# A matmul with bias and residual: own semaphores in one section, and one weight load for two matmuls

## The chip, the cores and the metric

The kernel runs on one core of a Trainium2 chip. The metric is the device time of one execution in microseconds (us); lower is better. Each kernel was run several times. A profiled execution also gives a span: the time from its first to its last instruction on the core. A difference of 2% (4.2 us here) or more is called faster or slower; anything less is "same".

## The reference

```python
batch, m, k, n = 16, 512, 1024, 768        # x and residual, weight and bias: random float32
def reference(x, weight, bias, residual):
    return (np.matmul(x, weight) + bias + residual).astype(np.float32)
```

That is 8192 rows of x, 64 tiles of 128 rows. In float32, x is 33.6 MB, the residual and the output are 25.2 MB each and the weight is 3.1 MB. So 87 MB have to move whatever the kernel does.

## The kernel before

Each tile of x is cast to bfloat16 by ScalarE (ACT). The TensorE (PE) transposes it in four pieces, with pairs of bfloat16 seen as one float32 word. VectorE (DVE) copies the transposed tile from PSUM to `XT`. Then 16 matmuls follow: eight slices of K, each with two column parts of W, 512 and 256 columns wide. GpSimd (POOL) adds the bias to the residual, and VectorE adds the PSUM result to that. All transfers are issued by SyncE (SP) on one queue.

```python
def mm(t, n0, nl, q, e):                        # called for both column parts, n0 = 0 and 512
    K_(nc.tensor.matmul(
        PO[t % HEAD][:, n0:n0 + nl], lhsT=XT[t % XT_N][:, q, :, e],
        rhs=w_sb[:, q, e, n0:n0 + nl],
        start=(q == 0 and e == 0), stop=(q == n_q - 1 and e == 1),
    ))
# ... cut ...
for t in range(HEAD, n_t):
    cast(t + 2)
    pool_adds(t + 1)
    transp(t + 1)
    if t < n_t - 1:
        for q in range(n_q):
            for e in range(2):
                for n0, nl in chunks:
                    mm(t, n0, nl, q, e)
    finish(t - 1)
    pool_adds(t + 1)
```

`nc.tensor.matmul` emits a weight load (of `lhsT`, the slice of x) and a matmul. So the same slice of x is loaded twice in a row, once for each column part. `K_` only keeps the order of the program; the framework sets all waits and semaphores. The framework also shares eight semaphores among all DMAs, so the ninth DMA waits until the first has landed.

## Time and profile before

| | kernel before |
|---|---|
| time, median of 3 runs | 211.56 us (211.50 to 211.57) |
| profiled run: time, span | 210.12 us, 208.3 us |
| TensorE matmul busy, weight loads busy | 97%, 62% |
| DMA engines busy, mean rate | 98.1%, 419 GB/s |
| granted TensorE clock | 0.996 |

"Busy" of the TensorE counts overlapping matmuls once, so 97% doesn't tell whether the matmuls are as dense as they can be. That has to be read from their spacing. PEld, the weight loads, is a row of its own because loads run beside matmuls. The lines are shown in the prediction below. Note that the profiled run (210.12 us) was 1.4 us quicker than the three timed ones; this turned out to matter.

### The profile page before, as it was taken

The numbers are of one execution on the slowest core, as the hardware profiler recorded it, in microseconds if no ns is written. First come the engines' busy times: TensorE is split into PE (matmuls) and PEld (weight loads), VectorE is DVE, ScalarE is ACT, GpSimd is POOL, SyncE is SP. The second block draws the span as 40 slices with busy tenths as digits, with TensorE's granted clock in tenths as the row PEclk, the third lists the DMA queues.
The fourth block names the chain that finished last, engine by engine and source line by source line (L and its number), as shares of the span: only waits on it lengthen the run. The fifth ranks groups of instructions, "written<-read, shape, count | busy, mean of one in ns | idle before, by whom it ended". The sixth has DMA issues, their size and how long they took to land.

```text
span 208.3 us, 3115 instructions
## 1 busy us (share of the span) xinstructions
PE 201.8 (97%) x1298; PEld 130.1 (62%) x1298; DVE 104.7 (50%) x140; ACT 66.1 (32%) x69; POOL 116.0 (56%) x72
## 2 busy tenths in 40 slices
PE   7899999999999999999999999999999999999991
PEld 2455666666666666666666666666666666666651
DVE  0457555445545544654554454555445545544542
ACT  2444513403640272420370094230092046430000
POOL 2100029759999905999029702999207950599500
PEclk9999999999999999999999999999999999999998
DMA  6999999999989999999999999999999999999995
GB/s 233 427 429 436 424 432 457 388 446 421 495 383 466 405 423 427 434 426 415 425 465 418 422 436 452 415 437 406 434 446 451 409 419 475 428 396 444 416 368 221
DMA packets 4927, 87.24 MB, mean 419 GB/s; under 512 B 557, under 2 KB 685, under 8 KB 1841
## 3 DMA queue, kind: packets, MB, share of 16 engines
q1 hardware_dynamic: 4913, 87.05, 98.1%
q8 instruction: 10, 0.16, 0.3%
q14 instruction: 4, 0.03, 0.0%
HBM read 61.88 MB, written 25.17 MB: 418 GB/s over the span
## 4 chain that ended last, share of the span: by engine, by line
PE 92%; DMA 4%; DVE 1%; SPq 0%; ACT 0%; issue 0%
PE psum_o L164 78%; PE pt L157 13%; DMA x_tile<-in_x_dram 4%; PE psum_o L258 1%; DVE xt L158 0%; ACT xb L146 0%; DVE ro L262 0%; SPq L119 0%; SPq L122 0%
## 5 line engine op out<-in xcount | busy, mean ns | idle before, releaser
L164 PE MATMUL psum_o<-w_sb,xt 128*128 128x512 bf16 x1008 | 174.0, 326 | 0.5 <-DVE xt L158 0.3
L164 PEld LDWEIGHTS <-xt 128*128 128x128 bf16 x1008 | 98.5, 98 | 59.2 <-DVE xt L158 0.7
L189 POOL TENSOR_TENSOR ro<-ro,bias_sb 128x768 f32<-128x768 f32 x50 | 88.9, 1823 | 48.2 <-DMA ro<-in_residual_dram 37.7
L149 ACT CAST xb<-x_tile 128x1024 bf16<-128x1024 f32 x60 | 59.7, 1043 | 113.9 <-DMA x_tile<-in_x_dram 74.1
L158 DVE COPY xt<-pt 128x1024 bf16<-128x1024 bf16 x64 | 44.1, 691 | 84.4 <-PE pt L157 84.4
L199 DVE TENSOR_TENSOR ro<-psum_o,ro 128x768 f32<-128x768 f32 x49 | 46.5, 948 | 4.6 <-POOL ro L189 3.4
L185 POOL TENSOR_TENSOR ro<-ro 128x768 f32<-128x768 f32 x14 | 25.0, 1820 | 25.0 <-DMA ro<-in_residual_dram 25.0
L157 PE MATMUL pt<-ident,xb 128*128 128x128 f32 x256 | 38.3, 273 | 0.6 <-DVE xb L149 0.4
L157 PEld LDWEIGHTS pt<-ident,xb 128*128 128x128 f32 x256 | 29.7, 140 | 9.0 <-ACT xb L146 1.1
L195 DVE TENSOR_TENSOR ro<-psum_o,bias_sb 128x768 f32<-128x768 f32 x14 | 13.2, 947 | 0.0
L208 PE MATMUL psum_o<-warm 128*128 128x512 bf16 x12 | 4.8, 587 | 1.2 <-DVE warm_a L204 1.2
L229 ACT CAST w_sb<-ro 128x768 bf16<-128x768 f32 x4 | 3.3, 832 | 3.7 <-DMA ro<-in_weight_dram 3.7
L208 PEld LDWEIGHTS <-warm 128*128 128x128 bf16 x12 | 1.6, 141 | 3.9 <-issue 2.7
L229 POOL CAST w_sb<-ro 128x768 bf16<-128x768 f32 x1 | 0.8, 824 | 5.5 <-DMA ro<-in_weight_dram 5.5
L149 DVE CAST xb<-x_tile 128x1024 bf16<-128x1024 f32 x1 | 0.7, 694 | 4.5 <-DMA x_tile<-in_x_dram 4.5
L146 ACT CAST xb<-x_tile 128x512 bf16<-128x512 f32 x3 | 1.8, 617 | 3.4 <-PE psum_o L164 1.7
L258 PE MATMUL psum_o<-w_sb,xt 128*128 128x512 bf16 (+1 forms) x16 | 2.8, 326 | 0.0
L229 DVE CAST w_sb<-ro 128x768 bf16<-128x768 f32 x3 | 1.7, 556 | 2.0 <-DMA ro<-in_weight_dram 2.0
L147 DVE CAST xb<-x_tile 128x512 bf16<-128x512 f32 x3 | 1.2, 424 | 2.6 <-DMA x_tile<-in_x_dram 2.6
L258 PEld LDWEIGHTS <-xt 128*128 128x128 bf16 x16 | 1.6, 98 | 1.1
L223 PE MATMUL psum_o<-warm 128*128 128x512 bf16 x6 | 1.6, 379 | 0.0
L262 DVE TENSOR_TENSOR ro<-psum_o,ro 128x512 f32<-128x512 f32 (+1 forms) x2 | 1.1, 557 | 0.9 <-PE psum_o L258 0.8
(14 smaller groups left out, 5.1 us busy)
## 6 DMA issues: line engine op xcount, KB each, us to landing
out_dram<-ro SPq DMA_DIRECT2D x3, 6144.0 KB, 34.1
x_tile<-in_x_dram SPq DMA_DIRECT2D x3, 5120.0 KB, 24.1
ro<-in_residual_dram SPq DMA_DIRECT2D x3, 3840.0 KB, 25.3
x_tile<-in_x_dram SPq DMA_DIRECT2D x3, 3072.0 KB, 40.2
ro<-in_residual_dram SPq DMA_DIRECT2D x3, 2304.0 KB, 17.5
x_tile<-in_x_dram SPq DMA_DIRECT2D x4, 1024.0 KB, 8.3
x_tile<-in_x_dram SPq DMA_DIRECT2D x2, 2048.0 KB, 21.0
out_dram<-ro SPq DMA_DIRECT2D x1, 3840.0 KB
```

The lines of the kernel that those rows point to most:

```text
L146: K_(nc.scalar.copy(out=dst[:, 0:K // 2], in_=src[:, 0:K // 2]))
L149: K_((nc.scalar.copy if how == "s" else nc.vector.tensor_copy)(out=dst, in_=src))
L157: K_(nc.tensor.transpose(out=pt[:, q, :], in_=words[:, ts(q, P)], identity=ident))
L158: K_(nc.vector.tensor_copy(out=XT[t % XT_N].rearrange("p q m e -> p (q m e)"), in_=pt.rearrange("p q m -> p (q m)").bitcast(BF16),))
L164: K_(nc.tensor.matmul(PO[t % HEAD][:, n0:n0 + nl], lhsT=XT[t % XT_N][:, q, :, e], rhs=w_sb[:, q, e, n0:n0 + nl], start=(q == 0 and e == 0) ...
L185: K_(nc.gpsimd.tensor_add(out=r, in0=r, in1=tmp(t)))
L189: K_(nc.gpsimd.tensor_add(out=r, in0=r, in1=bias_sb))
L195: K_(nc.vector.tensor_add(out=tmp(t), in0=p, in1=bias_sb))
L199: K_(nc.vector.tensor_add(out=row(t), in0=p, in1=row(t)))
L208: K_(nc.tensor.matmul(PO[0][:, 0:512], lhsT=warm[:, 0:P], rhs=warm, start=True, stop=True))
L229: K_(copy(out=w_sb[:, q, e, :], in_=w_st[:, 2 * q + e, :]))
L258: K_(nc.tensor.matmul(p, lhsT=XT[t % XT_N][:, q, :, e], rhs=w_sb[:, q, e, n0:n0 + nl], start=(q == 0 and e == 0), stop=(q == n_q - 1 and e ...
```

## The change

There are two intents. First, the program leaves the framework's semaphores: it records all operations with what they read and write, works out the smallest set of waits itself, gives each DMA a semaphore of its own, and emits everything inside one section for all engines. Second, in this form a weight load and its matmuls can be emitted separately, so a slice of x is loaded once for both column parts. The two belong together. I also built the kernel before with one explicit load and matmuls marked as having none. In its instruction list a load stood in front of every matmul all the same, beside the explicit one, so the framework's path puts them back. (That build was not run.)

```diff
+class Program:
+    def add(self, eng, emit, rd=(), wr=(), dma=False):      # records, with dependencies by key
+    def emit(self):                                          # ... cut: minimal waits ...
+            for d in waits[n]:
+                e.wait_ge(*mark[d])
+            ins = emit(e)
+            if dma:
+                sem = self.tc.alloc_semaphore(f"landed_{n}")
+                mark[n] = (sem, 16)
+                ins.then_inc(sem, 16)
+            elif n in told:
+                ins.then_inc(sems[eng], 1)                   # ... cut ...
-    def mm(t, n0, nl, q, e):
-        K_(nc.tensor.matmul(...))
+    def times(po, lhsT, rhs, first, final, rd, wr):
+        def emit(e):
+            return e.add_instruction(mybir.InstMatmult(..., ldweights=False))
+        op("pe", emit, rd, wr)
+    def mm(t, q, e, parts, po, wr):
+        lhsT, rd = XT[t % XT_N][:, q, :, e], [("XT", t % XT_N)]
+        op("pe", lambda g: g.ldweights(lhsT), rd)
+        for n0, nl, to in parts:
+            times(po[:, to:to + nl], lhsT, w_sb[:, q, e, n0:n0 + nl], ...)
+    # ... cut ...
-    K_(nc.gpsimd.memset(bias_row, 0.0))
+    fill("dve", bias_row, 0.0, "bias_row")
+    with tc.tile_critical():
+        prog.emit()
```

More of the change, by code (lines that the diff above doesn't have):

```diff
@@ L6 @@
 from concourse.bass import ts
-from concourse.masks import make_identity
 from concourse._compat import with_exitstack
@@ L38, with __init__ @@
 LAST = [(0, 512), (512, 256)]
+class Program:
+    def __init__(self, tc):
+        nc = tc.nc
+        self.nc, self.tc = nc, tc
+        self.engines = {"pe": nc.tensor, "dve": nc.vector, "act": nc.scalar, "pool": nc.gpsimd, "sp": nc.sync}
+        self.ops, self.writer, self.readers = [], {}, {}
+    def add(self, eng, emit, rd=(), wr=(), dma=False):
+        n, ops = len(self.ops), self.ops
+        deps = {self.writer[k] for k in (*rd, *wr) if k in self.writer and (eng != "pe" or ops[self.writer[k]][0] != eng)}
+        for k in wr:
+            deps.update(d for d in self.readers.get(k, ()) if ops[d][0] != eng or ops[d][3])
+        for k in rd:
+            self.readers.setdefault(k, set()).add(n)
+        for k in wr:
+            self.writer[k], self.readers[k] = n, set()
+        self.ops.append((eng, emit, deps - {n}, dma))
+    def emit(self):
+        ops, known = self.ops, {e: {} for e in self.engines}
+        lane, count, snap, waits = [], {}, [], []
+        for n, (eng, _, deps, dma) in enumerate(ops):
+            mine = (n, 0) if dma else (eng, count.setdefault(eng, 0) + 1)
+            if not dma:
+                count[eng] += 1
+            seen = known[eng]
+            need = {}
+            for d in deps:
+                f, i = lane[d]
+                if seen.get(f, -1) < i and i > need.get(f, (-1, 0))[0]:
+                    need[f] = (i, d)
+            need = {
+                f: (i, d) for f, (i, d) in need.items()
+                if not any(snap[d2].get(f, -1) >= i for g, (_, d2) in need.items() if g != f)
+            }
+            for f, (i, d) in need.items():
+                for g, v in (*snap[d].items(), (f, i)):
+                    if seen.get(g, -1) < v:
+                        seen[g] = v
+            waits.append([d for _, d in need.values()])
+            lane.append(mine)
+            own = dict(seen)
+            own[mine[0]] = mine[1]
+            snap.append(own)
+        told = {d for w in waits for d in w}
+        sems = {e: self.tc.alloc_semaphore(f"done_{e}") for e in self.engines if e != "sp"}
+        total, mark = dict.fromkeys(self.engines, 0), {}
+        for n, (eng, emit, _, dma) in enumerate(ops):
+            e = self.engines[eng]
+            for d in waits[n]:
+                e.wait_ge(*mark[d])
+            if emit is None:
+                continue
+            ins = emit(e)
[4 more added lines that the diff above has]
+            elif n in told:
+                total[eng] += 1
+                mark[n] = (sems[eng], total[eng])
+                ins.then_inc(sems[eng], 1)
@@ L58 @@
     n_t = M // P
-    n_s = n_t // J
     chunks = [(0, 512), (512, N - 512)]
@@ L84, with rows, dma @@
     (warm_a,) = fixed(sb, "warm_a", 1, [1, 2], FP32)
-    K_ = tc.keep_in_program_order
     w_st = R[:, W_ROW:W_ROW + 2 * n_q, :]
+    prog = Program(tc)
+    op = prog.add
+    def rows(a, b, cs=range(len(chunks))):
+        return [("R", r % RR, c) for r in range(a, b) for c in cs]
+    def dma(dst, src, rd, wr):
+        op("sp", lambda e: e.dma_start(out=dst, in_=src), rd, wr, dma=True)
     done = set()
     queue = list(ORDER)
+    stores = []
     def pump():
@@ L101, in pump @@
                 need = [("store", t - RR) for t in range(J * S + j0, J * S + j1) if t >= RR]
-                rows = [t % RR for t in range(J * S + j0, J * S + j1)]
-                if S < RR // J and any(W_ROW <= r < W_ROW + 2 * n_q for r in rows):
+                at = [t % RR for t in range(J * S + j0, J * S + j1)]
+                if S < RR // J and any(W_ROW <= r < W_ROW + 2 * n_q for r in at):
                     need.append(("wcast", n_q - 1))
                 if S < RR // J:
-                    need += [("add", t) for t in range(EARLY_END) if TMP_ROW + t in rows]
+                    need += [("add", t) for t in range(EARLY_END) if TMP_ROW + t in at]
             else:
@@ L111, in pump @@
             queue.pop(0)
+            t0, nj = J * S + j0, j1 - j0
             if kind == "b":
-                K_(nc.sync.dma_start(
-                    out=bias_row.rearrange("(g p) n -> g p n", p=QUAD)[:, 0, :],
-                    in_=bias[None, :].to_broadcast([P // QUAD, N]),
-                ))
+                dma(bias_row.rearrange("(g p) n -> g p n", p=QUAD)[:, 0, :],
+                    bias[None, :].to_broadcast([P // QUAD, N]), [], ["bias_row"])
                 continue
             if kind == "w":
-                K_(nc.sync.dma_start(out=w_st[:, 2 * S + j0:2 * S + j1, :], in_=w_d[:, S, j0:j1, :]))
+                dma(w_st[:, 2 * S + j0:2 * S + j1, :], w_d[:, S, j0:j1, :], [],
+                    rows(W_ROW + 2 * S + j0, W_ROW + 2 * S + j1))
                 continue
             if kind == "x":
-                K_(nc.sync.dma_start(out=X[:, (J * S + j0) % XR:(J * S + j0) % XR + j1 - j0, :], in_=x_d[S, :, j0:j1, :]))
+                dma(X[:, t0 % XR:t0 % XR + nj, :], x_d[S, :, j0:j1, :], [],
+                    [("X", t % XR) for t in range(t0, t0 + nj)])
             elif kind == "r":
-                K_(nc.sync.dma_start(out=R[:, (J * S + j0) % RR:(J * S + j0) % RR + j1 - j0, :], in_=res_d[S, :, j0:j1, :]))
+                dma(R[:, t0 % RR:t0 % RR + nj, :], res_d[S, :, j0:j1, :], [], rows(t0, t0 + nj))
             else:
                 n0, nl = (0, N) if kind == "s" else LAST[j1]
+                cs = range(len(chunks)) if kind == "s" else [j1]
                 j1 = j1 if kind == "s" else j0 + 1
@@ L129, in pump @@
                 for p0, p1 in zip(edges, edges[1:]):
-                    K_(nc.sync.dma_start(
-                        out=out_d[S, p0:p1, j0:j1, n0:n0 + nl],
-                        in_=R[p0:p1, (J * S + j0) % RR:(J * S + j0) % RR + j1 - j0, n0:n0 + nl],
-                    ))
+                    dma(out_d[S, p0:p1, j0:j1, n0:n0 + nl],
+                        R[p0:p1, t0 % RR:t0 % RR + j1 - j0, n0:n0 + nl], rows(t0, t0 + j1 - j0, cs), [("out", len(stores))])
+                    stores.append(("out", len(stores)))
                 done.update(("store", J * S + j) for j in range(j0, j1))
@@ L139, in mark, with copy, plus, fill @@
         pump()
+    def copy(eng, dst, src, rd, wr):
+        op(eng, lambda e: (e.copy if eng == "act" else e.tensor_copy)(out=dst, in_=src), rd, wr)
+    def plus(eng, dst, a, b, rd, wr):
+        op(eng, lambda e: e.tensor_add(out=dst, in0=a, in1=b), rd, wr)
+    def fill(eng, dst, v, wr):
+        op(eng, lambda e: e.memset(dst, v), [], [wr])
     def cast(t, how="s"):
@@ L143, in cast @@
             assert ("x", t) in done, t
-            src, dst = X[:, t % XR, :], XB[t % XB_N]
+            src, dst, h = X[:, t % XR, :], XB[t % XB_N], K // 2
+            rd, wr = [("X", t % XR)], [("XB", t % XB_N, i) for i in range(2)]
             if how == "sv":
-                K_(nc.scalar.copy(out=dst[:, 0:K // 2], in_=src[:, 0:K // 2]))
-                K_(nc.vector.tensor_copy(out=dst[:, K // 2:K], in_=src[:, K // 2:K]))
+                copy("act", dst[:, 0:h], src[:, 0:h], rd, wr[:1])
+                copy("dve", dst[:, h:K], src[:, h:K], rd, wr[1:])
             else:
-                K_((nc.scalar.copy if how == "s" else nc.vector.tensor_copy)(out=dst, in_=src))
+                copy("act" if how == "s" else "dve", dst, src, rd, wr)
             mark("cast", t)
@@ L153, in transp, with mm_all @@
         if t < n_t:
-            words = XB[t % XB_N].bitcast(FP32)
-            pt = PT[t % 2]
+            words, pt = XB[t % XB_N].bitcast(FP32), PT[t % 2]
             for q in range(n_q):
-                K_(nc.tensor.transpose(out=pt[:, q, :], in_=words[:, ts(q, P)], identity=ident))
-            K_(nc.vector.tensor_copy(
-                out=XT[t % XT_N].rearrange("p q m e -> p (q m e)"),
-                in_=pt.rearrange("p q m -> p (q m)").bitcast(BF16),
-            ))
-    def mm(t, n0, nl, q, e):
-        K_(nc.tensor.matmul(
-            PO[t % HEAD][:, n0:n0 + nl], lhsT=XT[t % XT_N][:, q, :, e],
-            rhs=w_sb[:, q, e, n0:n0 + nl],
-            start=(q == 0 and e == 0), stop=(q == n_q - 1 and e == 1),
-        ))
+                op("pe", lambda e, q=q: e.transpose(out=pt[:, q, :], in_=words[:, ts(q, P)], identity=ident),
+                   [("XB", t % XB_N, 2 * q // n_q), "ident"], [("PT", t % 2)])
+            copy("dve", XT[t % XT_N].rearrange("p q m e -> p (q m e)"),
+                 pt.rearrange("p q m -> p (q m)").bitcast(BF16), [("PT", t % 2)], [("XT", t % XT_N)])
+    def times(po, lhsT, rhs, first, final, rd, wr):
+        def emit(e):
+            return e.add_instruction(mybir.InstMatmult(
+                name=nc.get_next_instruction_name(),
+                ins=[e.lower_ap(rhs), e.lower_ap(lhsT, for_matmul_weights=True)], outs=[e.lower_ap(po)],
+                start_tensor_calc=first, stop_tensor_calc=final,
+                tile_size=(P, P), tile_position=(0, 0), ldweights=False,
+            ))
+        op("pe", emit, rd, wr)
[3 more added lines that the diff above has]
+        for n0, nl, to in parts:
+            times(po[:, to:to + nl], lhsT, w_sb[:, q, e, n0:n0 + nl], q == 0 and e == 0, q == n_q - 1 and e == 1,
+                  [*rd, ("w", q, e)], [wr])
+    def mm_all(t, qs):
+        for q in qs:
+            for e in range(2):
+                mm(t, q, e, [(n0, nl, n0) for n0, nl in chunks], PO[t % HEAD], ("PO", t % HEAD))
     def row(t, n0=0, nl=N):
@@ L182, in pool_adds @@
             adds.remove(t)
-            r = row(t)
+            r, rk = row(t), rows(t, t + 1)
             if t < EARLY_END:
-                K_(nc.gpsimd.tensor_add(out=r, in0=r, in1=tmp(t)))
+                plus("pool", r, r, tmp(t), rk + rows(TMP_ROW + t, TMP_ROW + t + 1), rk)
                 mark("add", t)
@@ L188, in pool_adds @@
             else:
-                K_(nc.gpsimd.tensor_add(out=r, in0=r, in1=bias_sb))
+                plus("pool", r, r, bias_sb, rk + ["bias"], rk)
                 mark("add", t)
     def finish(t):
-        p = PO[t % HEAD]
+        p, pk = PO[t % HEAD], ("PO", t % HEAD)
         if t < EARLY_END:
-            K_(nc.vector.tensor_add(out=tmp(t), in0=p, in1=bias_sb))
+            plus("dve", tmp(t), p, bias_sb, [pk, "bias"], rows(TMP_ROW + t, TMP_ROW + t + 1))
             mark("fin", t)
@@ L198, in finish, with dummies @@
             assert ("add", t) in done, t
-            K_(nc.vector.tensor_add(out=row(t), in0=p, in1=row(t)))
+            plus("dve", row(t), p, row(t), [pk] + rows(t, t + 1), rows(t, t + 1))
             mark("out", t)
-    K_(nc.vector.memset(warm, 0.0))
-    K_(nc.gpsimd.memset(bias_row, 0.0))
-    K_(nc.vector.memset(warm_a, 0.0))
-    K_(nc.scalar.copy(out=warm_a, in_=warm_a))
-    make_identity(nc, ident)
-    for _ in range(WARM):
-        K_(nc.tensor.matmul(PO[0][:, 0:512], lhsT=warm[:, 0:P], rhs=warm, start=True, stop=True))
-    def bias_rows():
-        K_(nc.vector.stream_shuffle(out=bias_sb, in_=bias_row, mask=[0] * QUAD))
+    def dummies(n, i):
+        for _ in range(n):
+            op("pe", lambda e: e.matmul(PO[i][:, 0:512], lhsT=warm[:, 0:P], rhs=warm, start=True, stop=True),
+               ["warm"], [("PO", i)])
+    fill("dve", warm, 0.0, "warm")
+    fill("dve", warm_a, 0.0, "warm_a")
+    fill("dve", bias_row, 0.0, "bias_row")
+    copy("act", warm_a, warm_a, ["warm_a"], ["warm_a"])
+    fill("pool", ident, 0.0, "ident")
+    op("pool", lambda e: e.affine_select(
+        out=ident, in_=ident, compare_op=mybir.AluOpType.not_equal, fill=1.0, base=0,
+        pattern=[[-1, P]], channel_multiplier=1,
+    ), ["ident"], ["ident"])
+    dummies(WARM, 0)
     pump()
@@ L215 @@
         if kind == "bias":
-            bias_rows()
+            op("dve", lambda e: e.stream_shuffle(out=bias_sb, in_=bias_row, mask=[0] * QUAD), ["bias_row"], ["bias"])
         elif kind == "cast":
@@ L221 @@
         elif kind == "warm":
-            for _ in range(a[0]):
-                K_(nc.tensor.matmul(PO[HEAD - 1][:, 0:512], lhsT=warm[:, 0:P], rhs=warm, start=True, stop=True))
+            dummies(a[0], HEAD - 1)
         elif kind == "tr":
@@ L227 @@
             q, e, eng = a
-            copy = {"v": nc.vector.tensor_copy, "s": nc.scalar.copy, "g": nc.gpsimd.tensor_copy}[eng]
-            K_(copy(out=w_sb[:, q, e, :], in_=w_st[:, 2 * q + e, :]))
+            r = W_ROW + 2 * q + e
+            copy({"v": "dve", "s": "act", "g": "pool"}[eng], w_sb[:, q, e, :], w_st[:, 2 * q + e, :], rows(r, r + 1), [("w", q, e)])
             if (q, e) == (n_q - 1, 1):
@@ L232 @@
         else:
-            for e in range(2):
-                for n0, nl in chunks:
-                    mm(a[0], n0, nl, a[1], e)
+            mm_all(a[0], [a[1]])
     pump()
@@ L246 @@
         if t < n_t - 1:
-            for q in range(n_q):
-                for e in range(2):
-                    for n0, nl in chunks:
-                        mm(t, n0, nl, q, e)
+            mm_all(t, range(n_q))
         finish(t - 1)
@@ L254 @@
     for i, (n0, nl) in enumerate(LAST):
-        p = PO[(t - 2 * (i % 2)) % HEAD][:, 512 * (i // 2):512 * (i // 2) + nl]
+        b = (t - 2 * i) % HEAD
         for q in range(n_q):
             for e in range(2):
-                K_(nc.tensor.matmul(
-                    p, lhsT=XT[t % XT_N][:, q, :, e], rhs=w_sb[:, q, e, n0:n0 + nl],
-                    start=(q == 0 and e == 0), stop=(q == n_q - 1 and e == 1),
-                ))
-        K_(nc.vector.tensor_add(out=row(t, n0, nl), in0=p, in1=row(t, n0, nl)))
+                mm(t, q, e, [(n0, nl, 0)], PO[b], ("PO", b))
+        plus("dve", row(t, n0, nl), PO[b][:, 0:nl], row(t, n0, nl), [("PO", b)] + rows(t, t + 1, [i]), rows(t, t + 1, [i]))
         mark("outc", i)
@@ L266 @@
     assert not queue, queue
+    op("sp", None, stores)
+    with tc.tile_critical():
+        prog.emit()
 _INS = ['x', 'weight', 'bias', 'residual']
```

## The prediction

> **What bounds the kernel now.** I read the profile's page first: busy shares, slices, queue table.
>
> ```profile
> PE 201.8 (97%) x1298; PEld 130.1 (62%) x1298; DVE 104.7 (50%) x140; ACT 66.1 (32%) x69; POOL 116.0 (56%) x72
> ...
> PE   7899999999999999999999999999999999999991
> ...
> DMA  6999999999989999999999999999999999999995
> ...
> q1 hardware_dynamic: 4913, 87.05, 98.1%
> ```
>
> Two resources are full from the second slice to the last but one: the TensorE and the 16 DMA engines. Weight loads (PEld) are 62% busy, but in a row of their own; whether they cost anything must be read from the spacing of the matmuls. For that I took the chain that ended last, in order of time (start us, us, what):
>
> ```profile
> 101.24 0.44 PE pt L157 x4
> 101.68 2.60 PE psum_o L164 x16
> 104.71 2.60 PE psum_o L164 x16
> 107.31 0.44 PE pt L157 x4
> ```
>
> From 104.71 to 107.75, where the next group of sixteen starts, one tile of 128 rows takes 3.04 us: 2.60 for its 16 matmuls (eight of 512 columns, eight of 256) and 0.44 for four transposes. At a granted clock of 1.00 and 2.4 GHz, 8 x (512 + 256) columns are 6144 / 2.4 = 2560 ns. The remaining 40 ns over 16 matmuls are 2.5 ns each. The weight load in front of each of the 16 therefore leaves no trace in the time beyond, at the most, those 2.5 ns. The third reading is the groups by form:
>
> ```profile
> L164 PE MATMUL psum_o<-w_sb,xt 128*128 128x512 bf16 x504 | 167.2, 379 | 0.5 <-DVE xt L158 0.3 <-ACT w_sb L229 0.2
> L164 PE MATMUL psum_o<-w_sb,xt 128*128 128x256 bf16 x504 | 137.4, 273 | 0.0
> ...
> L164 PEld LDWEIGHTS <-xt 128*128 128x128 bf16 x1008 | 98.5, 98 | 59.2 <-DVE xt L158 0.7 <-issue 0.6
> ```
>
> The matmuls of the main line sat idle for 0.5 us in all, and that in the head. A weight load takes 98 ns, less than the roughly 109 ns (256 / 2.4 + 2.5) for which a 256-column matmul occupies the array, so even the tightest pair hides it. The fourth reading is a table of stretches (PE, PEld, DVE, ACT, POOL busy, clock, DMA share, GB/s):
>
> ```profile
> 20.00:188.00 168.00, 168.00 (x1108) 110.71 (x1106) 87.46 (x113) 57.59 (x58) 106.46 (x60) 1.00 1.01 432
> 188.00:200.00 12.00, 12.00 (x82) 7.93 (x80) 6.08 (x9) 0.00 (x0) 7.35 (x5) 1.00 0.94 397
> 200.00:203.00 3.00, 3.00 (x18) 1.56 (x16) 1.40 (x2) 0.00 (x0) 0.00 (x0) 1.00 0.91 369
> 203.00:206.00 3.00, 1.05 (x9) 0.69 (x7) 1.11 (x2) 0.00 (x0) 0.00 (x0) 1.00 0.92 362
> 206.00:208.30 2.30, 0.00 (x0) 0.00 (x0) 0.00 (x0) 0.00 (x0) 0.00 (x0) 0.68 0.12 43
> ```
>
> In steady state the DMA moves 432 GB/s. A tile needs 512 KiB of x, 384 of residual and 384 of output, 1.31 MB, which at 432 GB/s is 3.03 us: the same as the 3.04 us of the TensorE. Neither can gain much without the other. Last, the waits of the DMA queue:
>
> ```profile
> SPq L292 <- DMA out_dram<-ro: 2.4, 1, 2.4
> ...
> SPq L281 <- PEq L281: 0.7, 1, 0.7
> SPq L292 <- PEq L292: 0.6, 2, 0.4
> ```
>
> The first DMA waits 0.7 us for the opening barrier; at the end the last small store costs 2.4 us to land, and then come closing waits and two barriers, about 1.0 us in all (the store landed near 207.3, the span ends at 208.3).
>
> **What the Trainium skill says.** "TensorE: Matmul & The Clock Gate", section "Wait — 56ns, not 53.3ns?", gives a warm start-to-start of N / 2.4 GHz + about 2.5 ns, called a fixed cost per matmul. The trace agrees: 8 x (215.8 + 109.2) = 2600 ns, the 2.60 above. The same page, "Step-by-step: what each phase is for", says that weight loads alone are pulled ahead of running matmuls into a background buffer; the 98 ns loads beside gapless matmuls agree. "Perfetto Trace Analysis", section "Identifying the Most-Contended Engine", takes the busy share of weight loads as a measure of headroom. Here it would mislead: 62% of loads, all hidden. "DMA: Bandwidth & Descriptors", section "Specifications", has a fabric ceiling of 435 GB/s; the 432 measured sits on it (its 358 GB/s for the HBM share of a core doesn't hold here).
>
> **The change, part by part.**
>
> (1) *One weight load for two matmuls.* In 63 tiles 8 of 16 loads go, 504 in all (the last tile keeps its 16, since it finishes its column parts one after the other). That is 504 x 98 ns = 49 us of PEld busy time, 130 to about 81 us, but none of it is on the path. The load that stays must hide behind the 256-column matmul, as it does today, and may even start during the 512-column one. What could be won is the 2.5 ns of the 256-column matmul if they were due to the change of weights: 504 x 2.5 = 1.3 us. The transposes speak against it: they too are spaced 0.44 us / 4 = 109 ns, which is the same law for another kind of operand, so I take the 2.5 ns as a cost of the matmul itself and give the gain a chance of one in three. Nor could all of it arrive. With the TensorE 1.3 us earlier, the stores come 1.3 us earlier at a DMA that is full. The room there is what it left idle between 188 and 203 us: estimated (432 - 397) x 12 + (432 - 369) x 3 = 609 kB, or 1.4 us. Much of that is likely to be the small rows of the last stores rather than waiting, so I allow about half, 0.7 us. Expected: 1/3 x 0.7 = 0.2 us off.
>
> (2) *Own semaphores.* Each DMA gets its own, instead of a few shared in turn, so the queue may be filled earlier: a load no longer waits for an earlier, unrelated transfer to land. But all DMAs are issued by one engine in the same order, and the DMA share is 1.0 from 12 us on; a deeper queue moves no byte sooner. The waits of the TensorE stay at two per tile (cast done, copy done), satisfied long before: the copy of a tile ends some 2 us before its matmuls. Expected: 0.0.
>
> (3) *The head.* The fill of the bias row moves from POOL (0.74 us) to the DVE, which is idle until the first x lands at 5.6 us; the identity is ready earlier, and nothing waits for it. The head is set by the order of x and W on the DMA, which doesn't change. Expected: 0.0.
>
> (4) *One section for all engines.* A fenced section has an entrance and an exit. If they work like the barriers of this trace, each is 0.3 to 0.4 us (0.7 us to the opening one with its set-up, 0.6 us for the two at the end). An entrance delays the first DMA, and so all that follows on a full DMA: estimated +0.2 us. At the exit there are eleven or so store semaphores to wait for instead of shared ones, mostly satisfied before the last lands, and one more synchronisation: +0.3 us.
>
> Sum: 211.56 - 0.2 + 0.0 + 0.0 + 0.2 + 0.3 = 211.86, which I round to **211.8 us**.
>
> **Rivals.** *A: the weight loads cost something after all.* Then the 504 removed loads give 1.3 us on the TensorE and the time falls to about 210.5. For it: the 2.5 ns might belong to the change of weights. Against it: the equal spacing of all kinds, and the full DMA. *B: a hidden load becomes exposed.* A separately written load might be ordered strictly after the matmul before it or lose its fast form. If each of the 8 per tile stood in the open for 98 ns, that were 63 x 8 x 98 ns = 49 us, near 260 us. Against it: the trace already has every load as an instruction of its own, beside the matmuls. Even a slow load, such as the transposes' 140 ns, has 325 ns of matmul to hide behind. *C: separate wait instructions bubble the TensorE.* Two waits per tile at an estimated 50 ns in the open would be 64 x 0.1 = 6.4 us, near 218. Against it: waits here are folded into instructions and the engine runs ahead. *D: the DMA is the true bound*, so that nothing in the middle matters; only the two ends count, and the time is 211.5 to 212.5. This one I hold for likeliest.
>
> **Range and chances.** The lower end takes rival A with the identity of both bounds loosened and a somewhat shorter end: 211.56 - 1.1 = 210.4. The upper takes a costlier entrance and exit, +0.9 each: 213.4. Faster by over 2% means below 207.4. With 87.05 MB at 432 GB/s, 201.5 us, plus about 2.5 us before the first bytes flow well, 2.7 us from the last issue to landing and 1 us to close, the span alone would be 207.7, and the time has been 3.3 us above the span. So 0.03. Slower by over 2% is above 215.8 and needs B or C: 0.06. Within: 0.91.
>
> **What would show it.** Right: PEld falls to about 794 instructions and 81 us, the sixteen matmuls still take 2.60 us, the tile 3.04; the DMA keeps 432 GB/s; differences sit before the first DMA and after the last store. If the sixteen take 2.58, A is right. If they take 2.7 or more, or idle time is put down to issue, B or C. Wrong altogether: a DMA rate in the middle other than 428 to 436 GB/s, for then a bound that I take as fixed has moved.

## The result

| | before | changed |
|---|---|---|
| time, median of 4 runs each | 211.53 us (211.41 to 211.57) | 210.91 us (210.71 to 211.18) |
| ratio, 95% interval | | 0.9973 (0.9955 to 0.9990): same |
| span of the profiled run | 208.3 us | 209.4 us |
| weight loads | 1298, 130.1 us | 794, 81.2 us |

A ratio is the mean time of one kernel's fast runs over the mean of the other's in the same rounds, so it is not quite the ratio of the medians beside it.

The time lies in the predicted range. But the time went down by 0.6 us while the profiled span went *up* by 1.1 us. Either the profile of the kernel before was not typical, or something happens outside the span.

From the page of the changed kernel (busy us, share and instructions of each engine; then busy tenths in 40 slices; then the queues):

```profile
PE 202.3 (97%) x1298; PEld 81.2 (39%) x794; DVE 105.3 (50%) x141; ACT 66.2 (32%) x69; POOL 115.2 (55%) x71
...
PE   7999999999999999999999999999999999999990
...
DMA  6999999999989899999999999999999999998993
...
q1 hardware_dynamic: 4913, 87.05, 97.6%
q8 instruction: 8, 0.13, 0.3%
```

Exactly 504 loads are gone and nearly 49 us of load time with them, yet both full rows, TensorE and DMA, look as before. The chain that ended last, in order of time:

```profile
101.28 0.44 PE pt L241 x4
101.72 2.60 PE psum_o L248 x16
104.31 0.44 PE pt L241 x4
104.75 2.60 PE psum_o L248 x16
107.35 0.44 PE pt L241 x4
```

The sixteen matmuls take 2.60 us and the tile 3.04, to the digit what they took with twice the loads. The groups by form (busy us, mean ns; idle before and its releaser):

```profile
L248 PE MATMUL psum_o<-w_sb,xt 128*128 128x512 bf16 x512 | 169.0, 379 | 0.3 <-DVE xt L217 0.3
L248 PE MATMUL psum_o<-w_sb,xt 128*128 128x256 bf16 x512 | 138.4, 273 | 0.0
...
L259 PEld LDWEIGHTS <-xt 128*128 128x128 bf16 x520 | 50.9, 98 | 102.5 <-issue 100.5 <-DVE xt L217 0.9
```

(520 are 63 x 8 plus the 16 of the last tile.) In the records of the trace the 256-column matmul starts 215.8 ns after the 512-column one, and the next one 109.2 ns after that, in both kernels. The table of stretches (PE, PEld, DVE, ACT, POOL busy, clock, DMA share, GB/s):

```profile
20.00:188.00 168.00, 168.00 (x1108) 67.36 (x663) 87.36 (x113) 57.60 (x58) 107.83 (x61) 1.00 1.01 432
188.00:200.00 12.00, 12.00 (x81) 4.86 (x48) 6.08 (x9) 0.00 (x0) 5.87 (x4) 1.00 0.97 414
200.00:203.00 3.00, 3.00 (x18) 1.19 (x13) 1.44 (x2) 0.00 (x0) 0.00 (x0) 1.00 0.87 349
203.00:206.00 3.00, 1.09 (x9) 0.69 (x7) 1.12 (x2) 0.00 (x0) 0.00 (x0) 1.00 0.94 372
```

The middle runs at the same 432 GB/s. What differs is the two ends. The first DMA of the kernel before, and that of the changed one (start us, us):

```profile
0.73 0.38 SPq L122 DMA_DIRECT2D x_tile<-in_x_dram  x1
```

```profile
0.95 0.39 SPq L159 DMA_DIRECT2D x_tile<-in_x_dram  x1
```

The section's entrance costs 0.22 us. At the other end, by the records of SyncE's waits, the kernel before sees its last store land at 207.27 and ends at 208.34, 1.07 us later. The changed kernel sees it at 207.74 and ends at 209.39, 1.65 us later: waits for the other stores, the section's own meeting of the engines, and a longer clearing of semaphores (0.29 us against 0.10). That is 0.58 us more. (The store itself lands 0.47 us later, though the last matmul ends at nearly the same time, 204.09 against 204.05.)

### The profile page after: what moved, and what is told of

It reads as the page before. It is cut to its first block, busy times and chain, and to the rows that moved or that the text cites. A ratio compares the mean times of both kernels' runs of the same rounds, so it can differ in the third digit from the quotient of the medians.

```text
span 209.4 us, 2487 instructions
## 1 busy us (share of the span) xinstructions
PE 202.3 (97%) x1298; PEld 81.2 (39%) x794; DVE 105.3 (50%) x141; ACT 66.2 (32%) x69; POOL 115.2 (55%) x71
## 4 chain that ended last, share of the span: by engine, by line
PE 92%; DMA 4%; DVE 1%; SPq 0%; ACT 0%; issue 0%
PE psum_o L248 79%; PE pt L241 13%; DMA x_tile<-in_x_dram 4%; SPq L159 0%; DVE xt L217 0%; ACT xb L217 0%; DVE ro L220 0%; SPq L390 0%; SPq L363 0%
## 5 line engine op out<-in xcount | busy, mean ns | idle before, releaser
L248 PE MATMUL psum_o<-w_sb,xt 128*128 128x256 bf16 (+1 forms) x1024 | 176.6, 326 | 0.3 <-DVE xt L217 0.3
L217 ACT CAST xb<-x_tile 128x1024 bf16<-128x1024 f32 (+1 forms) x63 | 61.4, 1023 | 117.1 <-DMA x_tile<-in_x_dram 81.8
L259 PEld LDWEIGHTS <-xt 128*128 128x128 bf16 x520 | 50.9, 98 | 102.5 <-issue 100.5
L220 DVE TENSOR_TENSOR ro<-psum_o,ro 128x768 f32<-128x768 f32 (+2 forms) x51 | 47.6, 934 | 6.3 <-POOL ro L220 4.3
L303 PE MATMUL psum_o<-warm 128*128 128x512 bf16 x18 | 6.9, 546 | 1.4 <-DVE warm_a L223 1.4
L217 DVE CAST xb<-x_tile 128x512 bf16<-128x512 f32 (+1 forms) x4 | 1.9, 492 | 5.8 <-DMA x_tile<-in_x_dram 5.8
L303 PEld LDWEIGHTS psum_o<-warm 128*128 128x128 bf16 x18 | 2.2, 127 | 4.7 <-issue 3.0
L320 DVE STREAM_SHUFFLE bias_sb<-bias_row 128x768 f32<-128x768 f32 x1 | 1.0, 1008 | 0.0
L223 DVE MEMSET bias_row<- 128x768 f32 x1 | 0.7, 698 | 0.1
```

The costliest lines, as they stand in the source:

```text
L217: op(eng, lambda e: (e.copy if eng == "act" else e.tensor_copy)(out=dst, in_=src), rd, wr)
L220: op(eng, lambda e: e.tensor_add(out=dst, in0=a, in1=b), rd, wr)
L223: op(eng, lambda e: e.memset(dst, v), [], [wr])
L248: return e.add_instruction(mybir.InstMatmult(name=nc.get_next_instruction_name(), ins=[e.lower_ap(rhs), e.lower_ap(lhsT, for_matmul_weight ...
L259: op("pe", lambda g: g.ldweights(lhsT), rd)
L303: op("pe", lambda e: e.matmul(PO[i][:, 0:512], lhsT=warm[:, 0:P], rhs=warm, start=True, stop=True), ["warm"], [("PO", i)])
```

## Experiments

Runs beside the same time of the kernel before were made on one chip in the same rounds: the first four on one chip, the last three on another. I call the two matmuls that share a slice of x "a pair".

| run | edit | mean us (runs) | before, same rounds | ratio (95%) |
|---|---|---|---|---|
| c_before | none, kernel before | 210.73 (6) | 211.27 (11) | 0.9972 (0.9951 to 0.9993) |
| c_after | none, changed kernel | 210.94 (6) | 211.27 | 0.9982 (0.9966 to 0.9998) |
| e_twoloads | two loads per pair | 212.05 (6) | 211.27 | 1.0037 (1.0011 to 1.0062) |
| e_lanes | DMA waits for the eighth before | 210.91 (5) | 211.27 | 0.9981 (0.9966 to 0.9995) |
| r_twoloads | two loads, repeated | 211.95 (6) | 211.07 (11) | 1.0045 (1.0032 to 1.0059) |
| e_threeloads | three loads per pair | 212.55 (6) | 211.07 | 1.0067 (1.0050 to 1.0084) |
| e_tail | few semaphores | 210.73 (6) | 211.07 | 0.9981 (0.9967 to 0.9995) |

### Controls: is there a difference at all?

No edit.

> Control: the kernel before, unchanged. The four runs of the changed kernel have their time 1.8 us above their span (211.18 - 209.4, 210.76 - 208.9 and so on), and so has the profiled run of the kernel before (210.12 - 208.3), but that run was 1.4 us faster than the other runs of the same kernel. Theory 1, the first profile was an unusually quick execution: the runs show times near 211.5 with spans near 209.7, and the extra 1.4 us can be found inside a trace. Rival, the section saves something outside the span: spans of 208.3 with times of 211.5.

> Control: the changed kernel, unchanged, beside the kernel before on one chip. Both theories: 210.9 us, spans 208.9 to 209.4, ratio 0.997. If the difference was between chips or by chance: 211.5, ratio 1.000.

Measured: the times of c_before were 210.32, 211.10, 210.11, 211.32, 210.26 and 211.26 us, with spans from 208.3 to 209.5. The gap between time and span was 1.8 us in all its runs and in those of c_after. So nothing is saved outside the span. The first profile of the kernel before had caught one of its quick executions (the six times above go quick and slow in turn); the difference of 3.3 us between time and span, on which the prediction leant, came from comparing two different executions. I had not expected the size of the spread: the kernel before against *itself* gives 0.9972, as far from 1 as the changed kernel gives (0.9973 and 0.9982). The 0.3% of the result is therefore not to be told from nothing. Where the quick and slow runs of the kernel before differ inside is not settled: both of its profiles, 208.3 and 208.5 us, are quick ones. The two profiles of the changed kernel, 209.4 and 209.1 us, differ after the last matmul: it ends at 204.09 and 204.17, the last store lands at 207.74 and 207.42.

### Are the loads free, and does the deeper queue matter?

```diff
 # e_twoloads
-        op("pe", lambda g: g.ldweights(lhsT), rd)
         for n0, nl, to in parts:
+            op("pe", lambda g: g.ldweights(lhsT), rd)
 # e_lanes
-        op("sp", lambda e: e.dma_start(out=dst, in_=src), rd, wr, dma=True)
+        lane = ("lane", len(lanes) % 8)              # lanes: a list, empty at first
+        lanes.append(lane)
+        op("sp", lambda e: e.dma_start(out=dst, in_=src), rd, [*wr, lane], dma=True)
```

> The changed kernel with the weight load put back before each of the two matmuls (only that part undone). Theory, the loads are hidden: PEld goes back from 81 to about 130 us busy and 1298 loads, sixteen matmuls still 2.60 us, time 210.9 within 0.3. Rival, the removed loads are the gain: 211.5, with the sixteen matmuls or idle time of the TensorE longer.

> The changed kernel, but each DMA is made to wait until the eighth before it has landed, as the shared semaphores of the kernel before make it do. Theory, a deeper queue moves no byte sooner: 210.9 within 0.3. Rival, the gain of 0.6 us comes from issuing DMAs earlier: 211.5, with the second to sixth x loads issued after 5.5 us again and the difference seen in when the early loads land.

Measured: e_lanes equals the changed kernel within the spread of runs (210.91 against 210.94). Its queue is held back again: the second 2 MB x load that the changed kernel issues at 6.17 us goes out at 10.04 (9.97 in the kernel before), and no change of the time follows. The deeper queue is worth nothing that these runs can show, as predicted.

e_twoloads was a miss for my theory: with the loads put back it is 1.1 us slower than the changed kernel (212.05 - 210.94), though its matmuls are spaced as before. I formed a new theory: the loads cost nothing on the TensorE but delay the DMA, which is full. To test it I repeated the run and added a third load.

### More loads

```diff
 # e_threeloads; r_twoloads is e_twoloads again
-        op("pe", lambda g: g.ldweights(lhsT), rd)
         for n0, nl, to in parts:
+            for _ in range(2 if to else 1):
+                op("pe", lambda g: g.ldweights(lhsT), rd)
```

> Repeat of the changed kernel with two loads, on another occasion. Theory, loads cost about 1 us and the section about 0.8 at its two ends: 0.3 to 0.5% above the kernel before. Rival, chance: between 0.997 and 1.001 of the kernel before.

> The changed kernel with three weight loads for each two matmuls: one before the 512-column matmul and two before the 256-column one, which have 216 ns to hide behind. Theory now (formed from the kernel with two loads, mean 212.05 us against 210.94 with one): each load takes something from the DMA, not from the TensorE. It expects another +1 us, about 213, with sixteen matmuls still 2.60 us. Rival, the two-load result was chance: 211 to 212, no trend with the number of loads. Third, the loads are serial and become visible: sixteen matmuls over 2.65 us and a time over 215.

Measured: the repeat holds, and the trend goes on: 210.94, 212.0 and 212.55 us with one, two and three loads per pair (the last +0.6 us, not the full +1 I expected). These are from two chips, but in the rounds of the repeat e_tail, which has one load, gave 210.73, so the step to two loads is there again. The sixteen matmuls still take 2.60 us. Where the time goes is seen in the chain of e_threeloads between 165 and 175 us (start us, us, what):

```profile
144.16 26.77 DMA x_tile<-in_x_dram
170.93 0.02 issue
170.95 1.05 ACT xb L217
172.00 0.04 issue
172.05 0.66 PE pt L241 x4
```

The TensorE waits for a transpose, which waits for a cast, which waits for x to land. The same cast in the control of the changed kernel, and then in e_threeloads:

```profile
169.83 1.99 ACT L217 CAST xb<-x_tile 128x1024 bf16<-128x1024 f32 x2 [12.29 <-DMA x_tile<-in_x_dram]
```

```profile
170.95 1.99 ACT L217 CAST xb<-x_tile 128x1024 bf16<-128x1024 f32 x2 [12.88 <-DMA x_tile<-in_x_dram]
...
172.05 0.55 PE L241 MATMUL pt<-ident,xb 128*128 128x128 f32 x3 [0.31 <-ACT xb L217]
```

With three loads this piece of x lands 1.1 us later. The records show how little room there is: the cast of tile 54 ends 0.43 us before its transposes start in the kernel before, 0.25 us in the changed kernel, and 0.23 and 0.16 us in their controls. A delay beyond this stops the TensorE. In the whole of e_threeloads it stops for 1.0 us in three places, in e_twoloads for 0.3 us in two, in r_twoloads nowhere.

The rest comes at the end. (Landings from here on are by their own records, up to 0.07 us before SyncE sees them.) Against the control of the changed kernel, the last matmul of e_twoloads ends 0.25 us later, the last store lands another 0.60 us later, and the exit takes 0.12 us more, together its 0.97 us of span. In e_threeloads these are 1.06, 1.09 and -0.13 us, in r_twoloads 0.02, 0.25 and 0.12 (its profiled run, 211.24 us, was the quickest of its six). With one load, too, the time from the last matmul to the last landing varies from 3.23 to 3.68 us in four profiles, so a single profile doesn't settle the second term. The exit's 0.12 us does not follow the loads: SyncE waits for the stores one after another, and behind the last landing the records show two more of these waits with one load, three with two and none with three.

The bytes show the delay itself. Summed over the packets of the queue, by 188 us the DMA had moved 79.43 to 79.52 MB in the four profiles of the section's kernels with one load, 79.36 MB in both with two, and 79.25 MB with three. At 432 GB/s the missing 0.1 and 0.2 MB are an estimated 0.3 and 0.5 us.

### The same kernels with room on the DMA

```diff
-                n0, nl = (0, N) if kind == "s" else LAST[j1]
+                n0, nl = (0, N // 2) if kind == "s" else LAST[j1]
```

Half of each output row is not stored, but for the last tile's (wrong result). About 12 MB fall away, and the DMA is no longer the bound.

> The kernel before with half of each output row stored for all but the last tile (wrong result on purpose), which takes about 12 MB from the 87 MB of transfers, so that the TensorE alone sets the pace. Reference for the next two: TensorE end near 203.8 us, time near 210, and less spread between runs than the 1.2 us of the full kernels if the DMA is what makes them vary.

> The changed kernel with the same half stores. Theory, the section costs 0.2 us at its entrance and 0.6 at its exit and sharing the loads gains nothing on the TensorE: 0.7 to 0.9 us above the kernel before with half stores. Rival, sharing the loads shortens the TensorE's own path by up to 1.3 us: equal or faster.

> The changed kernel with two loads and half stores. Theory, loads cost only through the saturated DMA, which here has room: within 0.2 us of the changed kernel with half stores. Rival, a second load costs about 1 us wherever it stands: 1 us above it.

| run, four runs each | loads per pair | mean us | lowest to highest |
|---|---|---|---|
| e_less_before | 2, no section | 209.22 | 209.10 to 209.35 |
| e_less_after | 1, section | 209.98 | 209.91 to 210.04 |
| e_less_twoloads | 2, section | 210.11 | 210.10 to 210.14 |

The DMA row of e_less_after, 40 slices:

```profile
DMA  6999999999999999999989999999999990006533
```

Three slices of zero, from 172 to 187 us: the DMA has done what there was and waits for the next stores. The spread of runs falls from 1.2 us to 0.25 or less, which speaks for the saturated DMA as what makes the full kernels vary. The section, with what comes along with it, costs 210.11 - 209.22 = 0.89 us. Sharing the loads saves 0.13 us, where it saved 1.1 us with the DMA full. In the traces even this small rest lies behind the last landing (1.67 us from there to the end with one load, 1.79 with two): the last matmul ends at 204.21 and 204.18 us, the last store lands at 206.56 and 206.53. Both fit the theory: a weight load has no cost to be seen on the TensorE's path, and it has one where the DMA has no room.

### Less work for the TensorE

```diff
-            mm_all(t, range(n_q))
+            mm_all(t, range(n_q - 1))      # and the stop flag one slice earlier
```

> The changed kernel without a quarter of the matmuls in 60 of 64 tiles (wrong result on purpose): 8 x 324 / 4 = 0.65 us less TensorE work per tile, 39 us in all. If the DMA is as much the bound as the TensorE, the span falls by 1.5 us at most, to about 207.5 or above, and the TensorE shows some 38 us of idle time put down to x loads. If the TensorE alone sets the pace, the span falls to about 170.

Measured: 212.23 us in one look, span 210.4, so not faster at all (wrong result on purpose; the granted clock averaged 0.95: in three stretches, each after waits of the TensorE, a 512-column matmul takes 427 ns to the next start instead of 216). Two stretches of time and the transposes:

```profile
20.00:188.00 168.00, 142.43 (x889) 59.48 (x565) 89.31 (x115) 57.28 (x58) 107.20 (x61) 0.96 1.01 431
188.00:200.00 12.00, 9.92 (x65) 4.57 (x46) 6.74 (x9) 0.00 (x0) 6.39 (x4) 1.00 0.97 418
```

```profile
L241 PE MATMUL pt<-ident,xb 128*128 128x128 f32 x256 | 40.4, 283 | 22.2 <-ACT xb L217 21.6 <-DVE xb L217 0.6
```

The DMA moves its 431 GB/s as before, and the freed time of the TensorE turns into waits for x. The busy time in the stretch fell by 25.6 us, and the page puts 22.2 us of idle time before the transposes, well short of the 38 I expected. Part of the rest is that the last matmul ends 6.1 us earlier (197.97 us against 204.09), part that matmuls at the lower clock take longer. The last store lands no earlier for it, at 208.65 us against 207.72. So the DMA alone needs the whole time. (It is one look of unknown state, and I draw nothing from its 1.3 us above the changed kernel.)

### The disputed cost by itself

```diff
-    chunks = [(0, 512), (512, N - 512)]
+    chunks = [(128 * i, 128) for i in range(6)]    # with a load before each
```

The start and stop flags were moved to the first and last 128 columns of each PSUM bank.

> The changed kernel with the 768 columns in six matmuls of 128 columns, each with its own weight load: the disputed cost by itself. If a load of 98 ns hides even behind a matmul of 128 columns: start-to-start 128 / 2.4 + 2.5 = 56 ns, eight groups of six in 8 x 6 x 56 = 2.69 us, the span some 5 us longer. If loads can follow one another only every 98 to 109 ns: 48 of them take 4.7 to 5.2 us per tile and the span grows to 330 us or more.[...]

Measured, result correct: 216.52 us, span 214.6. The chain and the weight loads:

```profile
102.21 2.68 PE psum_o L248 x48
104.89 0.44 PE pt L241 x4
105.33 2.68 PE psum_o L248 x48
```

```profile
L260 PEld LDWEIGHTS <-xt 128*128 128x128 bf16 x3040 | 175.5, 98 | 2.8 <-DVE xt L217 0.7 <-issue 0.3
```

Forty-eight matmuls of 128 columns, each with its own load of 98 ns, take 2.68 us, 55.8 ns each: 128 / 2.4 + 2.5. The loads, busy back to back, still hide. So a load overlaps not only the matmuls but also the next load, and 98 ns is its duration, not its spacing.

### A shorter exit

```diff
-                sem = self.tc.alloc_semaphore(f"landed_{n}")
-                mark[n] = (sem, 16)
+                # all stores count on one semaphore, loads on eight in turn; ... cut ...
+                mark[n] = (lanes[dma], 16 * lane[n][1])
```

> The changed kernel with few semaphores: all stores count on one, the loads on eight in turn. In the traces the time from the landing of the last store to the end of the span is 1.07 us in the kernel before (207.27 to 208.34) and 1.65 us in the changed one (207.74 to 209.39). Theory, part of that is the number of semaphores to wait for and to clear: the stretch shrinks to 1.2 to 1.3 us, the time by 0.3 us against the changed kernel, to about 0.996 to 0.997 of the kernel before. Rival, the stretch is the section's own exit: 1.6 us as before.

Measured: from the landing of the last store (207.57) to the end (208.93) it takes 1.36 us instead of 1.65, so half of the exit's extra goes (clearing the semaphores takes 0.14 us instead of 0.29). SyncE's wait for the last store is one wait now (us in total, times, longest):

```profile
SPq L371 <- DMA out_dram<-ro: 2.6, 1, 2.6
```

The time, 0.9981 of the kernel before, is the changed kernel's 0.9982: 0.3 us of 211 are below what the spread of runs lets one see. No version tried beats both kernels by a difference that the controls would not also show.

## Why the prediction was right, and where not

**The outcome** was right: 210.91 us, against 211.8 with a range of 210.4 to 213.4, and "within 2%". The forecast was for a slight loss and the medians show a slight gain, but the kernel before differs from itself by as much. That the number came so near is in part luck: the section cost 0.3 us more than predicted and the loads gave 0.9 us more, and these errors partly cancel.

**What bounds the kernel** was right. Rival D, which I held likeliest, is borne out by e_lesswork for its first half: a quarter of the matmuls less buys nothing (one run, and the TensorE is full as well: with half of the stores gone the time falls by 1 to 2 us only). "Only the two ends count" was its second half, and that fell, for the number of loads counts too.

**Part 1, the loads**, is where the sum failed, though the reading of the TensorE was right: 794 loads, 81.2 us, sixteen matmuls in 2.60 us, a tile in 3.04. The failing sentence is "none of it is on the path". It looked for the path on the TensorE alone and did not ask what the loads take from the DMA. Sharing the loads saved 1.1 us (e_twoloads against c_after; 0.1 of it is the order of the store waits in the exit), about the 1.3 us of rival A but not by its mechanism: the spacing did not move, and with room on the DMA only 0.13 us of the saving is left. The expected 0.2 us became 1.1. I also counted on up to 0.7 us of room at the DMA's tail. In e_lesswork the TensorE was done 6.1 us earlier and the last store landed no earlier, so there was none to be seen. Two slips in the working: rival A's 210.5 does not follow from its own terms (211.56 - 1.3 + 0.5 for the section is 210.8), and the transposes' 109 ns is what the law gives for 256 columns, while they have 128 (55.8 ns), so it was no support as it stood. The changed kernel supports it directly: the 256-column matmul starts the next one after 109.2 ns with or without a load of its own.

**Part 2, own semaphores**, was right: e_lanes, 210.91 against 210.94.

**Part 3, the head**, fits: in the traces the first cast starts at 5.60 us before and 5.75 after, a shift within the section's 0.22 us. It was not tested by itself.

**Part 4, the section**, was right in kind and too small. I had 0.2 at the entrance and 0.3 at the exit. The trace shows 0.22 and 0.58, together 0.80, and the half-store kernels show 0.89 in the time. In the full kernels, with two loads per pair, it is 212.05 - 211.27 = 0.78 and 211.95 - 211.07 = 0.88.

So the account of the full kernels is +0.78 for the section and -1.11 for the loads, -0.33 in sum (210.94 - 211.27). The sizes are rough, since they are differences of means and the control of the kernel before lies 0.54 us from the same kernel in its rounds; that the loads save is seen in two rounds on two chips (1.1 and 1.2 us), and the section's cost in three comparisons. Two effects of about a microsecond each hide behind "nothing happened".

**Rivals B and C** are refuted: no load is exposed, and in the changed kernel no matmul after the first 20 us starts late. Their 260 and 218 us stood far off.

**What stays open** is how a weight load delays the DMA. Two candidates were not separated. One is instruction fetching, which runs on the same DMA engines: with one, two and three loads the queue table counts 8, 10 and 12 instruction packets of 16 KB, each about 1 us of one engine. Two more of them are an estimated 0.13 us of sixteen engines, so they would have to count for more than their share, for instance because the program waits for all sixteen parts of a transfer. The other is the loads' own reads of SBUF. The e_six_each run has 26 such packets and 3314 loads, but its TensorE is slower, so its DMA had room again. A kernel with the same loads and a different number of instructions would tell.

## What to carry to other kernels

Before you cut work that is hidden on one engine, ask what else that work uses: here 504 of 1298 weight loads cost the TensorE nothing, and still about a microsecond where the DMA had no room left. When two resources are full, relieve one by a variant (half of the stores, fewer matmuls) and measure the change there; effects that drown in the spread of the full kernel become sharp. And run the kernel before against itself in the same rounds: a ratio of 0.997 with an interval that excludes 1 was what two copies of one kernel gave.

## What the Trainium skill lacked or had wrong

- "TensorE: Matmul & The Clock Gate", section "Back-to-back issue gap", gives some 81 ns per matmul of 128 columns and 131 ns per one of 512 for a stream of loads and matmuls. Here, with a load before each, they are 55.8 ns (e_six_each) and 215.8 ns (kernel before); N / 2.4 + 2.5 holds with and without loads.
- The same page, section "The mechanism", says in its list that a weight load overlaps running matmuls only in different row groups, though the paragraph above the list also allows loads into the background buffer. Here every load uses the full array, and 504 more of them moved no matmul, so the list's "only" does not hold.
- "Perfetto Trace Analysis", section "Identifying the Most-Contended Engine", takes the busy share of weight loads, beside the rate of arithmetic, as a measure of headroom. It stood at 93% in e_six_each with matmuls at full rate, and fell from 62% to 39% here without any change of pace.
- I found on no page that weight loads, hidden on the TensorE, delay a saturated DMA: 1.1 us for 504 loads, 0.13 us with room on the DMA, and that behind the last landing.
- I found on no page what a section for all engines costs: 0.22 us at the entrance and 0.58 us at the exit, of which 0.3 us go with fewer semaphores.
